# Four blocks of P in flight, half of the second token sums moved into the first products, and a later start for the sample tiles

## The chip, the cores and the metric

The kernel runs on one core of a Trainium2 chip. The metric is the device time of one execution in microseconds (us). The core has five engines with their own instruction queues: TensorE (PE in the profile, with the weight loads apart as PEld), VectorE (DVE), ScalarE (ACT), GpSimd (POOL) and SyncE (SP, which issues the transfers). Every engine takes its instructions in the order of the program, so one that waits holds up all that stand behind it.

## The reference

One layer of an encoder is computed for 1024 prompt tokens and 32 sample tokens with the same weights. Cut to what matters here:

```
h = x @ w_in                                  # q,k,v, indexer, retention q,k,v,gate, two gates
score = sum_h w[t,h] relu(q_idx . k_idx)      # then the top 256 keys of a query are kept
p = softmax(q k^T / 8 + bias, kept keys only) # 8 heads of 64
a = p @ v
o, S = retention_chunk(rotary(q), rotary(k), v, S)        # 8 heads, recurrent over chunks
m = sigmoid(g_a) * (a @ w_pa) + sigmoid(g_r) * (r @ w_pr)
x1 = layer_norm(alpha * x + m @ w_o)
h = silu(x1 @ w_gate) * (x1 @ w_up)           # D_FF = 2816 = 22 blocks of 128
y = layer_norm(alpha * x1 + h @ w_down)
```

## The kernel before

Nearly every product is done in three passes: an operand is split into a rounded high part and the low remainder, and the products high x high, high x low and low x high are summed. The helper `split` makes the two parts (L148 the high part on ACT, L152 the low part on POOL or DVE). In a `unit`, one 128x1024 piece of a weight is loaded and split.

The 1056 tokens are nine tiles, tiles 0 to 7 of 128 prompt tokens and tile 8 with the 32 sample tokens. The stages follow each other: the first projections with the indexer; keys and queries; the retention (`ret_job`); the sixteen gate blocks (`g_jobs`), into which the attention is woven; the merge (`c_jobs`); the output projection; the feed-forward (`u_plain`, then `u_jobs` with `products`); and the last projection.

TensorE's order is written out by hand. A planner, `Weave`, keeps a clock `W.t` of its own and planned busy times of ACT, DVE and POOL. A main generator yields its matmuls one by one; generators in `W.sides` are given the turn when the planned time at which they asked to go on has come. The order of the other engines is made by a scheduler from the data dependences, in a list schedule.

The three places of the change:

- **Retention.** `ret_job` projects a tile (q, k, v of two heads) and spawns `ret_tile`, which rotates q and k on POOL (L574 to L577, into `qk`), transposes both on PE (L580, L581), and goes on with products L593, L604, L607, L610 and the transposes L642. The time `t_ev` at which the projection should be evicted starts its plan. For the sample tile the projection is evicted by `merge_s` (ACT, then DVE L207 into `qkv`).
- **Attention.** `front` writes, for each head and tile, the scores (L788, L790), adds bias and mask (P<-TB,mask on POOL L778; sum and maximum on DVE L792), takes the exponential (ACT L802) and normalizes (DVE L805). `back` goes through blocks (head, group of two tiles, key block kb): it transposes a block of P into a PSUM bank (L842, L843; L849 for the sample tile), splits it into `ph` (ACT L148) and `pl` (DVE L152), and multiplies both with V (L866, L867; L872). `it - ia` is the number of blocks transposed and not yet multiplied. PE's PSUM tiles `m` come from a pool of six banks, `g` from one of two. The matmuls of the gate blocks (L172, `g<-xh`) are the main stream between them; the last gate block waits until the attention is done.
- **Feed-forward.** Blocks of the hidden layer are made two by two with seven products of sums instead of eight plain ones (`Quad` for the weights, `sums` for the tokens, `products` for the matmuls). The tokens are two halves of 528 columns, each in two parts `u` of 264. `sums(u)` makes, for four slices k, the sums `tq[1]`, `tq[2]`, `tq[3]` (tiles T) and `T4` (which takes the place of B12, a tile x) from B11, B12, B21, B22. `sums(0)` and `sums(1)` stand around the plain products of the first two blocks (`u_plain`, with SiLU on ACT L1168 and the product `sg` on DVE L1170). Then `products(q, 0, ...)` and `products(q, 1, ...)` run for each of 20 steps: seven groups of twelve matmuls, z = 0 to 6 (L1218). Group z = 0 is copied by ACT (L1222, `e1`) before group z = 4 may go on in the same bank; z = 1, 2, 3 are taken by DVE (L1224, L1226, L1228).

Of the kernel before, what the change touches and what calls it, by code (L numbers as in the profile page):

```python
# [104 lines left out]
def body(ctx, tc, nc, a):  # L105
# [20 lines left out]
    def f32(ap):  # L126
        return ap.bitcast(F32)
# [550 lines left out]
    def ret_job():  # L678
        for p in range(4):
            for t in range(9):  # L680
                if p == 3 and t == 1:
                    ring2.close()
                    st["hA"] = Open("headA")
                if p == 3 and 1 <= t < 6:
                    load_head(0, t - 1)
                if p < 3 and t < 4:
                    load_pair(p + 2, t)
                    W.on("v", 1.2, W.on("a", 0.95, W.t + 0.5))
                qkv = rp.tile([128, 512], F32, name="qkv", bufs=3)
                src = yield from nat_tile(units[p + 1], t, rp, qkv)  # L690
                t_ev = W.t + 0.2
                if t < 8:
                    nc.scalar.activation(qkv, src, AF.Copy)
                    t_ev = W.on("a", 0.5, W.t)
                    src = qkv
                W.spawn(ret_tile(p, t, src, t_ev))
            units.pop(p)
# [4 lines left out]
    def g_jobs():  # L702
        w = blk(unit(a["wT"][19], ring1, lo_eng="dve"))
        for b in range(16):
            cur = w
            if b < 15:
                w = blk(unit(a["wT"][20 + b], ring1, lo_eng="dve" if b < 1 else "pool"))
# [43 lines left out]
    def attention():  # L751
# [62 lines left out]
        def back():  # L814
# [4 lines left out]
            while ia < len(items):  # L819
                opts = []  # L820
                if it < len(items) and it - ia < 3:
                    h, g, kb = items[it]
                    opts.append((P_at.get((h, min(2 * g + 1, 8)), W.t + 0.3), 1))
# [9 lines left out]
                if is_t:  # L833
# [3 lines left out]
                    pt = mbank()  # L837
                    if g < 4:
                        ph = ap.tile([128, 256], F32R, name="ph", bufs=3)
                        pl = ap.tile([128, 256], F32R, name="pl", bufs=3)  # L840
# [5 lines left out]
                    else:  # L846
# [4 lines left out]
                        ph = ap.tile([128, 5, 2, 32], F32R, name="ps", bufs=1)  # L851
# [264 lines left out]
    def sums(u):  # L1116
        s = slice(u * SUB, (u + 1) * SUB)
        for k in range(4):
            a_, b_, c_ = (st["up"].tile([128, SUB], F32, name=nm, bufs=2) for nm in ("e1", "u2", "u3"))
            d_ = st["up"].tile([128, SUB], F32, name="ts", bufs=1)  # L1120
            nc.gpsimd.tensor_tensor(d_, f32(B21[0][:, k, s]), f32(B21[1][:, k, s]), op=ALU.add)
# [16 lines left out]
            nc.vector.tensor_tensor(c_, d_, c_, op=ALU.subtract)  # L1138
            cut(T4, c_)

    def u_plain():
# [29 lines left out]
        sums(1)  # L1171
# [80 lines left out]
    def u_jobs():  # L1252
        nxt = st["quad"]
        for x, (m, f) in enumerate(seq):
# [11 lines left out]
            yield from products(q, 0, sg, m == 0, {})  # L1266
# [209 lines left out]
```

## Time and profile before

| what | value |
|---|---|
| time, median of 3 runs | 1900.14 us (1900.13 to 1900.14) |
| the profiled execution | 1900.51 us |
| its span, first to last instruction | 1898.9 us |
| TensorE busy | 1859.0 us, 98% of the span |
| DVE, ACT, POOL busy | 68%, 38%, 40% |
| granted TensorE clock, mean | 0.994 of full |

The rows further down come from one profiled execution. A timeline row gives start and length in us, engine, line, operation, written tile <- read tiles, shapes and, in brackets, how long the engine had been idle and what ended the wait. Matmuls overlap, so the distance between two starts, not the length, tells what one costs.

### The profile page before, as it was taken

To read this page: it belongs to the slowest core of one execution; us is meant where nothing else is said; L and a number is where in the kernel's file an instruction comes from. 1 tells how busy PE (TensorE), PEld (TensorE's weight loads), DVE (VectorE), ACT (ScalarE), POOL (GpSimd) and SP (SyncE) were. 2 spreads that over 40 slices of the span, in tenths; PEclk is the share of its full clock that TensorE was granted. 3 is DMA by queue.
4 is the path that set the end of the run, shared out by engine and by line. 5 is a ranking of instruction groups with operands and counts; after the bars stand their busy time and mean duration, and the time that the engine had idled before them with its cause. 6 is when DMAs were issued, how large, how long until landed. Compare 5 with 4: busy or idle time off the path is not lost. (4 is left out here: it accounts for less than half of the span.)

```text
span 1898.9 us, 31028 instructions
## 1 busy us (share of the span) xinstructions
PE 1859.0 (98%) x11361; PEld 1688.2 (89%) x11361; DVE 1298.4 (68%) x2693; ACT 715.1 (38%) x1495; POOL 751.8 (40%) x787
## 2 busy tenths in 40 slices
PE   8999999999999999999999999899999999999998
PEld 8999899787888999998999879899999999877776
DVE  4599889999995776676533378754555555476667
ACT  5443322423333555555522255432333332432212
POOL 5445633455545544543321133243343333462211
PEclk9999999999999999999999999999999999999999
DMA  5335742223334756551845662212222222642212
GB/s 189 113 128 196 266 138 86 65 73 98 87 86 125 195 144 171 143 145 52 273 146 155 186 199 84 67 68 67 80 96 71 75 82 90 203 165 89 83 40 91
DMA packets 154367, 233.11 MB, mean 123 GB/s; under 512 B 18960, under 2 KB 118280, under 8 KB 154216
## 3 DMA queue, kind: packets, MB, share of 16 engines
q1 hardware_dynamic: 147736, 223.03, 37.6%
q10 hardware_dynamic: 6480, 8.11, 1.3%
q8 instruction: 89, 1.46, 0.3%
q14 instruction: 62, 0.51, 0.1%
HBM read 164.79 MB, written 67.48 MB: 122 GB/s over the span
## 5 line engine op out<-in xcount | busy, mean ns | idle before, releaser
L152 POOL TENSOR_TENSOR wlo<-raw,whi 128x1024 fp32r<-128x1024 f32 (+2 forms) x83 | 196.1, 2367 | 337.8 <-ACT whi L148 295.2
L148 ACT ACTIVATE whi<-raw 128x1024 fp32r<-128x1024 f32 (+1 forms) x158 | 137.1, 881 | 183.8 <-PE m L1218 33.7
L172 PE MATMUL g<-xh,whi 128*128 128x384 f32 (+1 forms) x600 | 198.2, 330 | 0.0
L172 PE MATMUL g<-xl,whi 128*128 128x384 f32 (+1 forms) x600 | 198.1, 330 | 0.0
L172 PE MATMUL g<-xh,wlo 128*128 128x384 f32 (+1 forms) x600 | 197.9, 330 | 0.0
L377 DVE MAX8 m<-sc 128x8 f32<-128x384 f32 (+6 forms) x209 | 182.2, 874 | 4.7
L378 DVE MATCH_REPLACE8 sc<-m,sc 128x384 f32<-128x384 f32 (+6 forms) x209 | 180.0, 862 | 0.1
L778 POOL TENSOR_TENSOR P<-TB,mask 128x512 f32<-128x512 f32 (+3 forms) x112 | 99.1, 913 | 120.9 <-PE m L842 98.3
L172 PEld LDWEIGHTS g<-xl,whi 128*128 128x128 f32 x600 | 113.5, 189 | 3.0 <-issue 0.9
L172 PEld LDWEIGHTS g<-xh,wlo 128*128 128x128 f32 x600 | 113.5, 189 | 2.4 <-issue 0.5
L172 PEld LDWEIGHTS g<-xh,whi 128*128 128x128 f32 x600 | 113.5, 189 | 2.2
L1315 DVE TENSOR_TENSOR yo<-m,yo 128x512 f32<-128x512 f32 x128 | 85.4, 686 | 43.5 <-PE m L172 42.1
L1218 PE MATMUL m<-T,whi 128*128 128x264 f32 x624 | 114.6, 283 | 0.0
L172 PE MATMUL g<-whi,xl 128*128 128x512 f32 x256 | 104.9, 410 | 0.0
L172 PE MATMUL g<-whi,xh 128*128 128x512 f32 x256 | 104.4, 408 | 0.0
L172 PE MATMUL g<-wlo,xh 128*128 128x512 f32 x256 | 104.4, 408 | 0.0
L1218 PEld LDWEIGHTS m<-T,whi 128*128 128x128 f32 x624 | 96.6, 188 | 0.0
L172 PE MATMUL m<-rT,whi 128*128 128x384 f32 (+1 forms) x384 | 90.7, 322 | 0.0
L1218 PE MATMUL m<-T,wlo 128*128 128x264 f32 x312 | 88.6, 284 | 0.0
L1218 PE MATMUL g<-x,whi 128*128 128x264 f32 x416 | 79.2, 287 | 5.6 <-ACT e L1222 5.6
L1218 PE MATMUL m<-x,whi 128*128 128x264 f32 x416 | 78.5, 287 | 1.2 <-DVE u L1226 0.7
L152 DVE TENSOR_TENSOR wlo<-raw,whi 128x512 fp32r<-128x512 f32 (+1 forms) x81 | 69.6, 872 | 14.0 <-ACT whi L148 13.1
(333 smaller groups left out, 5493.4 us busy)
## 6 DMA issues: line engine op xcount, KB each, us to landing
raw<-wT SPq DMA_DIRECT2D x33, 512.0 KB, 3.7
raw<-w_gate SPq DMA_DIRECT2D x22, 512.0 KB, 3.4
raw<-w_up SPq DMA_DIRECT2D x22, 512.0 KB, 3.4
hd<-sg SPq DMA_DIRECT2D x22, 512.0 KB, 3.2
raw<-w_down SPq DMA_DIRECT2D x22, 512.0 KB, 3.5
raw<-hd SPq DMA_DIRECT2D x22, 512.0 KB, 3.6
raw<-wr SPq DMA_DIRECT2D x16, 512.0 KB, 4.2
ml<-mtd SPq DMA_DIRECT2D x16, 512.0 KB, 4.5
```

The costliest lines, as they stand in the source:

```text
L148: nc.scalar.activation(hi, src, AF.Copy)
L152: e.tensor_tensor(lo, src, f32(hi), op=ALU.subtract)
L172: nc.tensor.matmul(out, lhsT=l, rhs=r, start=i == 0, stop=i == m - 1)
L377: nc.vector.max(m8[0:n], v)
L378: nc.vector.match_replace(v, m8[0:n], v, TAKEN)
L778: nc.gpsimd.tensor_tensor(pp[0:n, n0:n0 + nn], TB[0:n, b0 + n0:b0 + n0 + nn], masks[t][0:n, n0:n0 + nn], op=ALU.add)
L1218: nc.tensor.matmul(o, lhsT=w[l][:, k, :], rhs=b[r][:, k, s], start=z < 4 and k == 0 and j == 0, stop=k == 3 and j == 2, skip_group_check=True)
L1315: nc.vector.tensor_tensor(y, src, y, op=ALU.add)
```

## The change

```diff
@@ ret_job, after the projection of tile t
                     src = qkv
+                else:
+                    t_ev += 1.6
                 W.spawn(ret_tile(p, t, src, t_ev))
@@ g_jobs
-                w = blk(unit(a["wT"][20 + b], ring1, lo_eng="dve" if b < 1 else "pool"))
+                w = blk(unit(a["wT"][20 + b], ring1, lo_eng="dve" if b < 2 else "pool"))
@@ attention, back()
-                if it < len(items) and it - ia < 3:
+                if it < len(items) and it - ia < 4:
                     h, g, kb = items[it]
-                    opts.append((P_at.get((h, min(2 * g + 1, 8)), W.t + 0.3), 1))
+                    opts.append((max(P_at.get((h, min(2 * g + 1, 8)), W.t + 0.3), tev.get(it - 3, 0.0) - 0.6), 1))
...
                     pt = mbank()
+                    pp = ap.tile([128, 512], F32R, name="ph", bufs=4)
                     if g < 4:
-                        ph = ap.tile([128, 256], F32R, name="ph", bufs=3)
-                        pl = ap.tile([128, 256], F32R, name="pl", bufs=3)
+                        ph, pl = pp[:, 0:256], pp[:, 256:512]
...
-                        ph = ap.tile([128, 5, 2, 32], F32R, name="ps", bufs=1)
+                        ph = pp[:, 0:320].rearrange("p (b i c) -> p b i c", b=5, i=2)
@@ sums
-    def sums(u):
+    def sums(u, ks=range(4)):
         s = slice(u * SUB, (u + 1) * SUB)
-        for k in range(4):
+        for k in ks:
             a_, b_, c_ = (st["up"].tile([128, SUB], F32, name=nm, bufs=2) for nm in ("e1", "u2", "u3"))
-            d_ = st["up"].tile([128, SUB], F32, name="ts", bufs=1)
-            nc.gpsimd.tensor_tensor(d_, f32(B21[0][:, k, s]), f32(B21[1][:, k, s]), op=ALU.add)
...
-            nc.vector.tensor_tensor(c_, d_, c_, op=ALU.subtract)
+            whole(b_, B21)
+            nc.vector.tensor_tensor(c_, b_, c_, op=ALU.subtract)
             cut(T4, c_)
@@ u_plain, behind the plain products
-        sums(1)
+        sums(1, range(2))
@@ u_jobs
-            yield from products(q, 0, sg, m == 0, {})
+            yield from products(q, 0, sg, m == 0, {z: (lambda k=z: sums(1, [k + 1])) for z in (1, 2)} if x == 0 else {})
             yield from products(q, 1, sg, m == 0, hooks)
```

The sample tile's `ret_tile` is planned 1.6 us later; the low part of the weight piece of gate block 2 (piece 21) goes from POOL to DVE; four blocks instead of three may be transposed ahead, the fourth not before the splits of the block three earlier are planned to end, less 0.6 us; the sum over B21 is made on DVE (`whole`) instead of POOL; and slices k = 2 and 3 of `sums(1)` are written behind groups z = 1 and z = 2 of the first products.

**POOL at the fourth sample tile.** The rows are POOL's rotation of the last sample tile (`qk_6609`) and the low parts `wlo` of gate weights that stand next to it. Before:

```order
L574 TENSOR_TENSOR qk_6609<-qkv_6514,rot_6604 32x256
L575 TENSOR_TENSOR t2_6610<-qkv_6514,rot_6604 32x256
L152 TENSOR_TENSOR wlo_6819<-raw_6816,whi_6818 128x1024
L576 TENSOR_TENSOR qk_6609<-qk_6609,t2_6610 32x4x32
L577 TENSOR_TENSOR qk_6609<-qk_6609,t2_6610 32x4x32
L152 TENSOR_TENSOR wlo_6948<-raw_6945,whi_6947 128x1024
```

The same place in the changed kernel:

```order
L574 TENSOR_TENSOR qk_6609<-qkv_6514,rot_6604 32x256
L575 TENSOR_TENSOR t2_6610<-qkv_6514,rot_6604 32x256
L576 TENSOR_TENSOR qk_6609<-qk_6609,t2_6610 32x4x32
L577 TENSOR_TENSOR qk_6609<-qk_6609,t2_6610 32x4x32
L152 TENSOR_TENSOR wlo_6921<-raw_6918,whi_6920 128x1024
```

The weight's low part that stood inside the rotation is gone from POOL's queue; it is now made by DVE.

**PE at the end of the attention.** The rows are the transposes of blocks of P into PSUM tiles `m`, and their products with V; the block transposed into `m_N` is split into `ph_(N+1)`. Before, for the last head:

```order
L842 MATMUL m_10921<-ident_65,P_10732 128x128
L843 MATMUL m_10921<-ident_65,P_10796 128x128
L866 MATMUL m_10928<-ph_10900,V_9876 128x256
L867 MATMUL m_10928<-pl_10901,V_9876 128x256
L842 MATMUL m_10931<-ident_65,P_10732 128x128
L843 MATMUL m_10931<-ident_65,P_10796 128x128
L866 MATMUL m_10928<-ph_10909,V_9876 128x256
L867 MATMUL m_10928<-pl_10910,V_9876 128x256
L842 MATMUL m_10940<-ident_65,P_10732 128x128
L843 MATMUL m_10940<-ident_65,P_10796 128x128
L866 MATMUL m_10928<-ph_10922,V_9876 128x256
```

In the changed kernel, from the last matmul of gate block 15 on (the last but one of the sixteen):

```order
L172 MATMUL g_10681<-xh_141,wlo_10174 128x288
L844 MATMUL m_10745<-ident_65,P_10534 128x128
L845 MATMUL m_10745<-ident_65,P_10587 128x128
L868 MATMUL m_10694<-ph_10685,V_9739 128x256
L869 MATMUL m_10694<-ph_10685,V_9739 128x256
L844 MATMUL m_10753<-ident_65,P_10534 128x128
L845 MATMUL m_10753<-ident_65,P_10587 128x128
L868 MATMUL m_10694<-ph_10700,V_9739 128x256
L869 MATMUL m_10694<-ph_10700,V_9739 128x256
L844 MATMUL m_10761<-ident_65,P_10534 128x128
L845 MATMUL m_10761<-ident_65,P_10587 128x128
L868 MATMUL m_10694<-ph_10711,V_9739 128x128
```

Between a block's transposes and its first product stood the products of two other blocks, and now stand those of three. Behind the last matmul of that gate block 85 rows of the attention were left, and now 41 are (the whole list of PE's rows was counted).

**ACT ahead of the first products.** The rows are the high parts of the second token sums (T, x), of the hidden block for the sample tokens (`hs`), and the copy `e1` of group z = 0. Before:

```order
L148 ACTIVATE hs_13240<-sg_13268 128x32
L148 ACTIVATE T30_13533<-u2_13888 128x264
L148 ACTIVATE T30_13533<-u2_13908 128x264
L148 ACTIVATE T20_13531<-u3_13889 128x264
L1222 ACTIVATE e1_13970<-g_13966 128x264
L148 ACTIVATE T20_13531<-u3_13909 128x264
L148 ACTIVATE x10_01_12441<-u3_13889 128x264
L1231 ACTIVATE sg_13944<-g_13966 128x264
```

In the changed kernel:

```order
L148 ACTIVATE hs_13080<-sg_13108 128x32
L1223 ACTIVATE e1_13764<-g_13760 128x264
L148 ACTIVATE T10_13369<-e1_13793 128x264
L148 ACTIVATE T30_13373<-u2_13794 128x264
L148 ACTIVATE T20_13371<-u3_13795 128x264
L1243 ACTIVATE sg_13738<-sg_13738 128x264
L1232 ACTIVATE sg_13738<-g_13760 128x264
```

The copy now follows `hs` directly; the three high parts that stood between them come later.

## Rows read from the trace of the kernel before

**Rows 1.** The page, busy time of each engine.
```profile
PE 1859.0 (98%) x11361; PEld 1688.2 (89%) x11361; DVE 1298.4 (68%) x2693; ACT 715.1 (38%) x1495; POOL 751.8 (40%) x787
```
**Rows 2.** Waits of PE, whole span (total, times, longest).
```profile
PE m L580 <- POOL qk L577: 5.8, 3, 2.8
PE g L1218 <- ACT e L1222: 5.6, 1, 5.6
...
PE m L1218 <- DVE u L1226: 1.1, 4, 0.5
```
**Rows 3.** Timeline of PE at 448 us, one sample tile.
```profile
448.32 0.24 PE L580 MATMUL m<-ident,qk 32*128 32x32 f32 x1 [1.91 <-POOL qk L577]
...
449.36 0.40 PE L172 MATMUL g<-wlo,xh 128*128 128x512 f32 x1
449.59 0.39 PE L172 MATMUL g<-whi,xl 128*128 128x512 f32 x1
```
**Rows 4.** Timeline of POOL at 585 us, the last sample tile.
```profile
584.86 2.35 POOL L152 TENSOR_TENSOR wlo<-raw,whi 128x1024 fp32r<-128x1024 f32 x1 [0.26 <-ACT whi L148]
587.17 0.45 POOL L576 TENSOR_TENSOR qk<-qk,t 32x128 f32<-32x128 f32 x1
```
**Rows 5.** Waits of PE from 626 to 879.5 us, the attention.
```profile
PE m L867 <- DVE pl L152: 2.4, 5, 0.9
PE m L866 <- ACT ph L148: 0.8, 1, 0.8
PE m L788 <- DVE mx L792: 0.5, 2, 0.2
```
**Rows 6.** Stretches: length, busy us (instructions) PE, PEld, DVE, ACT, POOL; clock, DMA.
```profile
879.53:900.85 21.32, 16.75 (x93) 13.28 (x91) 16.46 (x51) 12.87 (x33) 3.67 (x3) 0.84 0.14 40
...
883.80:890.60 6.80, 5.94 (x21) 4.71 (x22) 5.48 (x18) 2.83 (x7) 0.20 (x1) 0.50 0.30 87
...
900.85:904.25 3.40, 3.40 (x12) 3.40 (x12) 0.40 (x2) 0.22 (x1) 0.00 (x0) 0.50 0.10 22
...
1164.00:1204.40 40.40, 40.40 (x335) 40.40 (x334) 39.10 (x91) 20.14 (x46) 14.33 (x10) 1.00 0.21 79
...
1204.40:1210.40 6.00, 5.99 (x50) 5.77 (x48) 4.09 (x4) 2.52 (x5) 5.85 (x5) 1.00 0.00 0
...
1204.43:1223.47 19.04, 12.97 (x87) 12.45 (x85) 13.78 (x29) 6.61 (x16) 6.57 (x6) 0.82 0.08 28
...
1214.90:1221.70 6.80, 5.25 (x22) 4.94 (x23) 4.79 (x13) 3.00 (x8) 0.75 (x1) 0.50 0.07 21
```
**Rows 7.** Timeline of POOL and DVE at 736 us, in the attention.
```profile
736.44 2.56 POOL L152 TENSOR_TENSOR wlo<-raw,whi 128x1024 fp32r<-128x1024 f32 x1 [3.46 <-ACT whi L148]
...
736.66 2.35 DVE L800 TENSOR_TENSOR mx<-mx 128x1 f32<-128x1 f32 x1
```
**Rows 8.** Timeline of PE and DVE at 897 us, blocks of the last head.
```profile
897.03 0.27 PE L843 MATMUL m<-ident,P 128*128 128x128 f32 x1
...
897.49 0.27 PE L843 MATMUL m<-ident,P 128*128 128x128 f32 x1
...
897.76 0.88 DVE L152 TENSOR_TENSOR pl<-m,ph 128x256 fp32r<-128x256 f32 x2 [0.38 <-ACT ph L148]
...
898.24 0.39 PE L867 MATMUL m<-pl,V 128*128 128x256 f32 x1
```
**Rows 9.** Timeline of DVE, ACT and PE, 1206 to 1216 us, the first products.
```profile
1206.43 1.50 DVE L1138 TENSOR_TENSOR u<-ts,u 128x264 f32<-128x264 f32 x1 [1.91 <-POOL ts L1121]
...
1212.10 0.42 DVE L1170 TENSOR_TENSOR sg<-m,sg 128x264 f32<-128x264 f32 x1
1212.44 0.42 DVE L1124 TENSOR_TENSOR u<-x,x 128x264 f32<-128x264 f32 x1
...
1215.56 0.37 ACT L1222 ACTIVATE e<-g 128x264 f32<-128x264 f32 x1
...
1215.99 0.81 PE L1218 MATMUL g<-x,whi 128*128 128x264 f32 x2 [5.60 <-ACT e L1222]
```

## The prediction

> **What bounds the kernel now.** I read the page first: TensorE is busy 1859.0 of 1898.9 us [rows 1], so the time can fall only where PE waits, or where it works at half clock. The waits of PE name the places [rows 2]: three waits for the rotated sample tile (5.8 us, the longest 2.8), one wait of 5.6 us for the copy `e1` at the first products, and small ones of 1.1 us there. The waits of the attention come in two stretches: 3.7 us in the long one, where gate matmuls stand between the blocks [rows 5], and 4.6 us of idle time in the 21.3 us at its end, where none are left [rows 6]. The stretches also give the granted clock [rows 6]: it stands at 0.50, the lower of the two levels (1.2 instead of 2.4 GHz), in 883.8 to 890.6, in 900.85 to 904.25 and in 1214.9 to 1221.7 us, each time behind one of these waits. So a wait costs its length and often some us at half speed behind it. The change touches just these places.
>
> **Sample tiles of the retention.** The sum of the three waits is 5.8 us; the longest is 2.8 [rows 2], the middle one 1.91 [rows 3], so the first is 1.1. The wait ends when POOL has rotated `qk`. Putting the plan 1.6 us later moves PE's other work ahead of the transposes. In the second of these tiles 22 projection matmuls instead of 16 and two more transposes stand between the end of the sample projection and its transposes (counted in the order); at 0.23 us each [rows 3] the six are 1.4 us, with the transposes about 1.5, and 0.4 us of the 1.91 stay. In the first tile four matmuls and one product L593 come ahead, about 1.2 us against 1.1: nothing stays. In the last tile POOL's `wlo` of 2.35 us stood between the second and the third step of the rotation, and its third step began only at 587.17 [rows 4]; this row is gone from there, and eight more matmuls stand ahead, so the 2.8 us go wholly. The low part now costs DVE about 1.2 us (an estimate: half of POOL's 2.35), hidden as long as the product that waits for DVE stands more than that behind its turn; the order keeps some 3.6 us of other matmuls between L593 and L604, as before. Later tiles are spaced as before within 0.1 us at the shortest, so I add no new wait. Term: 5.8 - 0.4 = **5.4 us**, between 4.2 (0.6 us left in each of two tiles, 0.4 in a third) and 5.8.
>
> **First products.** From their start to the start of the second part (`u` = 1) they took 19.04 us. At full clock 50 matmuls take 6.00 us, 0.12 each, so the 84 of one part are 10.1 us: 8.9 us were lost there (the wait of 5.6, some 0.5 of small waits, and 2.8 at half clock) [rows 2, 6]. The cause is a chain of late work. DVE was busy 39.10 of the 40.40 us ahead [rows 6], and came 7.5 us late to the last `sg`, at 1212.10, when PE had ended its product at about 1204.6; on the way it also waited 1.91 us for POOL's `ts` [rows 9]. Behind `sg` the order gives ACT three high parts of the second sums, which wait for DVE in turn, before `e1`, which came at 1215.56 [rows 9].
>
> After the change `e1` stands right behind `hs`. Ahead of the last `sg` DVE has as many rows as before, 94 against 95: the eight sums over B21 replace what of slices 2 and 3 stood there. Counted with the distance of two starts, 0.34 us [rows 9], they are about 35 us of work; in the trace the same rows kept DVE busy some 45 us (39.1 up to 1204.4, and 5.8 of the 7.7 us to the last `sg`), because DVE instructions stretch while POOL works (the row of 1.50 us with POOL's name beside it is a 0.42 us one [rows 9]). Five of POOL's ten rows there [rows 6] are `ts`, so I let 6 of these 10 us stay: DVE, which begins at about 1165.5, reaches the last `sg` at about 1206.7, `e1` comes at 1207.5, and group z = 4 needs it at 1204.4 + 4 x 1.45 = 1210.2. If all 10 us stay, it comes at 1211.2 and PE waits 1.0 us. Then slices 2 and 3: 24 DVE rows and what they wait for end near 1216.9, and the second part reads the last slice of `tq[2]` at 1204.4 + 10.1 + 1.45 + 1.1 = 1217.1. There the cover is thin. ACT must first copy the second part's `e1`, ready at 1216.1, before the last high part; I put 0.6 us of new waiting here, and up to 2.5 if DVE is late by all the 10 us. Without such waits the clock has no reason to fall. Term: 8.9 - 0.6 = **8.3 us**, between 5.4 (1.0 and 2.5 us come back) and 8.9.
>
> The Trainium skill bears on this step: its page "SBUF — State Buffer" (Who interferes with whom) says that a DVE instruction with two SBUF inputs contends with a GpSimd instruction that reads SBUF, and that the second to issue is blocked. By that rule the sum over B21 is no safer on DVE than on POOL, and POOL's remaining weight sums could hold it up; the trace agrees that a DVE row with SBUF inputs alone can stand 2.35 us where POOL works [rows 7]. It would move this term towards 5.4.
>
> **Attention, its end.** From the last gate matmul to the end PE was busy 16.75 of 21.32 us: 4.57 us idle. In the two stretches at half clock it was busy 5.94 and 3.40 us, of which half, 3.0 and 1.7, is the price of the clock [rows 6]. Together 9.3 us. From a block's second transpose to its product with the low part it was 1.21 us [rows 8], and before the change a block had only about 0.9 us of PE work in between. After it, 41 instead of 85 rows lie behind the last gate matmul, no scores among them, and three blocks' work (about 1.3 us) stands between transpose and product. A block follows the next on PE in 0.46 us and costs DVE 0.44 [rows 8], so the splits just keep up. I leave 1.2 us for its last, short blocks, and expect no fall of the clock. Term: **8.0 us**, between 5.0 (the longer fall returns) and 9.3.
>
> **Attention, its long part.** The 3.7 us of waits [rows 5] come where POOL splits a gate weight: 2.56 us of POOL, a DVE row of one column stretched to 2.35 beside it, and the splits `pl` behind it late [rows 7]. Thirteen such POOL rows stay. A fourth block in flight gives a block more cover where there was least of it; over all blocks the median of PE work between transpose and product goes only from 3.05 to 3.26 us. The price of such a hit is not known in the new order. It can be anything from nothing (all 3.7 us won) to 1.5 us more than now (two more hits of the size of the longest ones, 0.8 and 0.9 us). Term: **1.8 us**, half.
>
> **The sum.** 5.4 + 8.3 + 8.0 + 1.8 = 23.5 us. The profiled execution took 1900.51 us, its span is 1.6 us shorter, and the median of the runs is 0.4 us below it; I subtract from the median: 1900.1 - 23.5 = **1876.6 us**. All low ends together give 13.1 us (1887.0), all high ends 27.7 us (1872.4).
>
> **The rivals.**
>
> The attention gives nothing back (chance 0.15): the fourth block changes the order, new hits by POOL's splits take the place of the old ones, and the end keeps its waits and its falls of the clock. For it speaks that POOL's rows are all still there; against it that 44 rows have left the bare end. Then 13.7 us of gain remain: 1886.4.
>
> The end of the attention stays dense but the clock falls in it anyway (0.15). Between the two falls the clock was full for ten us of transposes and products, since the mean of 0.84 over the end is just the first fall, and it fell again right behind them [rows 6]; so the trace doesn't exclude it. As a mechanism of this kernel: transposes are half of these rows; if they keep the clock no better than idle time, one or two falls return, at 1.7 to 3.0 us, and 1876.6 becomes 1878.3 to 1881.3. The Trainium skill, "TensorE: Matmul & The Clock Gate" (Part 4: PE-mode transpose), says that a transpose doesn't count as busy in the same way; by that rule this rival holds.
>
> The second sums are late (0.12): DVE is late by all that POOL took from it, and the products of the second part wait for slice 3. 3.5 us come back, 1879.5 (2.9 above the forecast), a little more if the clock falls again.
>
> The fourth block takes a PSUM bank (0.03), and the kernel is slower. Six banks hold two score tiles, up to two sums over V and now four transposed blocks. If the scores have to wait for the fourth block's splits, the nearest row is 0.23 us each (0.5 us in two waits for DVE's `mx` [rows 5]); with 112 score pieces that is 26 us against 23.5: 1902. It decides from about 100 of the 112 on. Against it: the fourth is held back in the plan, and in the order a bank's next use lies at least as far behind as before.
>
> No change that can be measured (0.03): the waits only move, 1900.
>
> **How the numbers follow.** The forecast itself has 0.52. Its own range is 1873 to 1880; the clock rival and the late sums lie within 1878 to 1882, the first rival at 1886. A range of 1871.5 to 1887 leaves out some 0.15: the two last rivals and a gain beyond the high ends. Less than 0.2% (3.8 us) can hardly be told from no change here. Faster by more has 0.94, the same 0.03, slower 0.03.
>
> **What would show it.** Right: no wait of PE for `qk` above 0.6 us; POOL's last rotation without a split inside; `e1` before 1210 us on the old clock and no wait of over a us in the first products; about 8 us instead of 21 from the gate matmul at the attention's bare end to its last product; clock 1.00 through both places. Wrong: a wait for T or `x` in the second part of the first products, waits for `pl` in the long part above 4 us together, or score products that wait for `mx` many times.

## The result and the profile after

The changed kernel takes 1877.4 us (median of four runs, 1875.5 to 1878.5); the kernel before took 1900.1 us beside it. The ratio on record is 0.9864, with a 95% interval of 0.9847 to 0.9882, so it is faster; the two medians alone give 0.9880, which lies in the interval. The forecast was 1876.6 us. One execution of run 5 below, 2082.6 us at a mean clock of 0.82, was slow and counts in no ratio. The profiled execution took 1878.54 us, with a span of 1876.4 us, 22.5 less than the 1898.9 before.

The page, busy time of each engine (answers to [rows 1]):

```profile
PE 1852.4 (99%) x11361; PEld 1681.8 (90%) x11361; DVE 1293.0 (69%) x2702; ACT 713.4 (38%) x1495; POOL 741.5 (40%) x778
```

PE is busy 6.6 us less though it executes the same number of instructions. Most of that is half clock that is gone: half of PE's busy time at 0.50 was 7.3 us before and is 1.7 now. The other 15.9 of the 22.5 us are waiting. The waits of PE over the whole span (total, times, longest; answers to [rows 2]):

```profile
PE m L306 <- ACT xh L148: 4.3, 1, 4.3
...
PE m L869 <- DVE ph L152: 1.3, 1, 1.3
PE m L844 <- DVE mx L794: 1.1, 1, 1.1
...
PE m L580 <- POOL qk L577: 0.6, 1, 0.6
PE m L1219 <- ACT T L148: 0.5, 1, 0.5
```

The wait of 5.6 us for `e1` is no longer there, and of the three waits for `qk` (5.8 us) one of 0.6 is left. New are a wait of 1.3 us for a split of P, one of 1.1 us for `mx`, and 0.5 us for T. The stretches of the changed kernel (columns as in [rows 6]) show where the half clock went:

```profile
754.06:757.47 3.41, 3.41 (x15) 3.31 (x15) 0.90 (x3) 1.10 (x4) 2.92 (x4) 0.50 0.01 2
879.34:886.17 6.83, 6.14 (x49) 5.37 (x48) 3.88 (x12) 5.05 (x14) 2.38 (x1) 1.00 0.35 107
1187.97:1198.10 10.13, 10.13 (x86) 10.12 (x85) 9.06 (x24) 5.03 (x13) 1.59 (x2) 1.00 0.16 53
```

The second row is the bare end of the attention: 6.83 us with 0.7 us of idle time and a clock of 1.00, against 21.32 us with 4.57 idle, 6.8 of them at 0.50, and 3.4 more at 0.50 right behind, before. It also holds fewer rows, 49 against 93. The third is the way from the first products to the start of their second part: 10.13 us without a gap, against 19.04. The first row is new: 3.41 us at half clock in the attention's long part. Before, three stretches were at half clock (6.8, 3.4 and 6.8 us [rows 6]) between the kernel's start and its last microseconds; this one is all that is left there.

The places of [rows 4] and [rows 9] again, in the changed kernel. POOL rotates the last sample tile without a pause, and the low part of a weight comes later:

```profile
580.59 0.72 POOL L574 TENSOR_TENSOR qk<-qkv,rot 32x256 f32<-32x256 f32 x1 [2.21 <-PE m L604]
581.28 0.73 POOL L575 TENSOR_TENSOR t<-qkv,rot 32x256 f32<-32x256 f32 x1
582.09 0.45 POOL L576 TENSOR_TENSOR qk<-qk,t 32x128 f32<-32x128 f32 x1
582.51 0.45 POOL L577 TENSOR_TENSOR qk<-qk,t 32x128 f32<-32x128 f32 x1
585.22 2.38 POOL L152 TENSOR_TENSOR wlo<-raw,whi 128x1024 fp32r<-128x1024 f32 x1 [2.26 <-ACT whi L148]
```

And DVE, ACT and PE in the first products:

```profile
1191.07 0.42 DVE L1171 TENSOR_TENSOR sg<-m,sg 128x264 f32<-128x264 f32 x1
...
1191.65 0.37 ACT L1223 ACTIVATE e<-g 128x264 f32<-128x264 f32 x1
...
1201.43 0.39 PE L1219 MATMUL m<-T,mh 128*128 128x264 f32 x1 [0.55 <-ACT T L148]
...
1202.12 0.39 PE L1219 MATMUL m<-T,mh 128*128 128x264 f32 x1 [0.31 <-DVE T L152]
```

The first products now start at 1187.97 instead of 1204.43, 16.5 us earlier; on the old clock `e1` comes at 1208.1, before group z = 4 needs it at 1210.2, and PE doesn't wait. It waits later, 0.86 us in two waits for the last slice of `tq[2]`. By the distance of the starts these two cost 1.3 us: the start of the second part comes 25.4 us earlier than before (1198.10 against 1223.47), the row at 1202.12 only 24.0 (1226.16 before).

The new wait in the long part, with the fall of the clock behind it, has this history on POOL, DVE and PE:

```profile
748.80 2.39 POOL L152 TENSOR_TENSOR wlo<-raw,whi 128x1024 fp32r<-128x1024 f32 x1 [5.67 <-ACT whi L148]
...
749.75 1.59 DVE L807 TENSOR_SCALAR P<-P,mx 128x256 f32<-128x256 f32 x1
...
752.49 1.27 DVE L152 TENSOR_TENSOR ph<-m,ph 128x256 fp32r<-128x256 f32 x4
...
752.96 0.38 PE L869 MATMUL m<-ph,V 128*128 128x256 f32 x1 [1.31 <-DVE ph L152]
```

POOL splits a gate weight for 2.39 us. Beside it, a DVE row over 256 columns takes 1.59 us, though the same operation over 640 columns took 0.54 us at 736 us in the kernel before. The low parts of P behind it are late, and PE waits 1.31 us. It is the pattern of [rows 7] at another place.

### The profile page after: what moved, and what is told of

Its sections match the earlier page's. It is cut to its first block, busy times and chain, and to the rows that moved or that the text cites. A ratio compares the mean times of both kernels' runs of the same rounds, so it can differ in the third digit from the quotient of the medians.

```text
span 1876.4 us, 30959 instructions
## 1 busy us (share of the span) xinstructions
PE 1852.4 (99%) x11361; PEld 1681.8 (90%) x11361; DVE 1293.0 (69%) x2702; ACT 713.4 (38%) x1495; POOL 741.5 (40%) x778
## 5 line engine op out<-in xcount | busy, mean ns | idle before, releaser
L172 PE MATMUL g<-xl,whi 128*128 128x384 f32 (+1 forms) x600 | 198.7, 331 | 0.0
L172 PE MATMUL g<-xh,wlo 128*128 128x384 f32 (+1 forms) x600 | 198.0, 330 | 0.0
L172 PE MATMUL g<-xh,whi 128*128 128x384 f32 (+1 forms) x600 | 197.4, 329 | 0.0
L172 PEld LDWEIGHTS g<-xl,whi 128*128 128x128 f32 x600 | 113.2, 189 | 3.1 <-issue 0.9
L172 PEld LDWEIGHTS g<-xh,wlo 128*128 128x128 f32 x600 | 113.3, 189 | 2.7 <-issue 0.5
L172 PEld LDWEIGHTS g<-xh,whi 128*128 128x128 f32 x600 | 113.1, 189 | 2.6
L172 PE MATMUL g<-wlo,xh 128*128 128x512 f32 x256 | 105.3, 411 | 0.0
L172 PE MATMUL g<-whi,xh 128*128 128x512 f32 x256 | 105.0, 410 | 0.0
L172 PE MATMUL g<-whi,xl 128*128 128x512 f32 x256 | 103.4, 404 | 0.0
L172 PE MATMUL m<-rT,whi 128*128 128x384 f32 (+1 forms) x384 | 90.8, 322 | 0.0
L1199 POOL TENSOR_TENSOR raw<-raw,qs 128x512 f32<-128x512 f32 x20 | 31.9, 1596 | 145.5 <-DVE wlo L152 95.0
L794 DVE CUSTOM_DVE_ANT_0 P<-m,P 128x512 f32<-128x512 f32 (+3 forms) x112 | 59.0, 532 | 38.6 <-PE m L792 34.3
L152 DVE TENSOR_TENSOR ph<-m,ph 128x256 fp32r<-128x256 f32 (+2 forms) x176 | 62.0, 374 | 28.7 <-ACT ph L148 27.7
```

The source lines that it names most:

```text
L152: e.tensor_tensor(lo, src, f32(hi), op=ALU.subtract)
L172: nc.tensor.matmul(out, lhsT=l, rhs=r, start=i == 0, stop=i == m - 1)
L794: nc.vector.tensor_tensor_reduce(out=pp[0:n, n0:n0 + nn], in0=L[0:n, 0:nn], in1=pp[0:n, n0:n0 + nn], scale=1.0, scalar=-3e38, op0=ALU.add, ...
L1199: nc.gpsimd.tensor_tensor(a12, a12, self.s2, op=ALU.subtract)
```

## The experiments

Twelve runs were made, of eleven other kernels and of the changed one again, each in up to five rounds beside the kernel before. That one took 1898.7 to 1907.2 us in the 37 runs of these rows, with medians of 1903.1, 1902.7 and 1903.8 us, so differences from the kernel before are given against the median of the same row. Runs 1 to 4, 5 to 8 and 9 to 12 are one row each; a comparison across rows is given by the times and by the ratios, which need not agree. All ratios are to the kernel before, with 95% intervals.

**Run 1: the sample tiles alone.** The kernel before with

```diff
+                else:
+                    t_ev += 1.6
                 W.spawn(ret_tile(p, t, src, t_ev))
-                w = blk(unit(a["wT"][20 + b], ring1, lo_eng="dve" if b < 1 else "pool"))
+                w = blk(unit(a["wT"][20 + b], ring1, lo_eng="dve" if b < 2 else "pool"))
```

> Only the later plan of the sample tiles and gate piece 21's low part on DVE. If the three parts of the change are independent: the three waits for qk (5.8 us) shrink to 0.6, nothing else moves, 1900.1 - 5.2 = 1894.9 us. Rival, the parts lean on each other: the 30 gate matmuls that are pulled ahead of the sample tiles are missing in the attention (860 instead of 890 stand inside it in the order), and with three blocks in flight 97 instead of 84 rows lie behind the last gate matmul. At the 9.3 us that the bare end cost for 84 rows, 0.11 each, 1.4 us come back: about 1896.3, and a longer bare end with the same falls of the clock.

Measured: 1893.9 us, 9.3 below before; ratio 0.9951 (0.9937 to 0.9964). This is more than either theory gave. The waits of PE:

```profile
PE m L845 <- DVE P L807: 4.2, 1, 4.2
...
PE m L580 <- POOL qk L577: 0.6, 1, 0.6
```

The waits for `qk` shrink as expected, by 5.2 us. The end of the attention keeps its idle time (one wait alone takes 4.2 us), with less half clock than in the profile of before:

```profile
875.21:878.62 3.41, 2.81 (x10) 2.62 (x11) 3.10 (x14) 2.99 (x7) 1.37 (x2) 0.50 0.20 44
```

Here 3.4 us stand at 0.50 where before has 10.2, and in the first products 3.4 us where before has 6.8. As half of PE's busy time, these falls cost 2.9 instead of 7.3 us. So 4.4 of the 9.4 us by which the two spans differ were gained at places that the edit doesn't touch, and the falls of one kernel vary between executions: the runs of the kernel before have mean clocks of 0.991 to 0.995.

But the profile of before may also show too few falls at the sample tiles. In the five other kernels of this study in which the sample tiles' plan is that of before (runs 2, 3, 5, 6 and 11), each profile shows half clock at a wait for `qk`, from its last half microsecond on or behind it. Stretches of run 3 and the wait ahead of the first:

```profile
448.08 0.25 PE L580 MATMUL m<-ident,qk 32*128 32x32 f32 x1 [1.90 <-POOL qk L577]
```

```profile
449.03:452.44 3.41, 3.41 (x11) 2.61 (x10) 3.41 (x8) 0.69 (x3) 0.00 (x0) 0.50 0.40 147
588.98:595.80 6.82, 6.19 (x20) 5.68 (x21) 4.46 (x7) 2.06 (x7) 4.67 (x7) 0.50 0.65 218
```

Runs 3 and 5 had both falls, 10.2 us at half clock, which cost 4.8 and 4.6; runs 2, 6 and 11 had one of 3.4 us, which cost 1.6 to 1.7. The mean over the five is 2.9 us. The one profile of before on which the prediction was worked out has the same waits [rows 2, 3] and no fall behind them. With the 5.2 us of the waits themselves that makes 8.1 us, inside the measured interval of 6.9 to 12.0. How much of the 9.3 us the sample tiles gave is not shown.

**Run 2: the fourth block alone.** The kernel before with

```diff
-                if it < len(items) and it - ia < 3:
+                if it < len(items) and it - ia < 4:
...
-                    opts.append((P_at.get((h, min(2 * g + 1, 8)), W.t + 0.3), 1))
+                    opts.append((max(P_at.get((h, min(2 * g + 1, 8)), W.t + 0.3), tev.get(it - 3, 0.0) - 0.6), 1))
...
+                    pp = ap.tile([128, 512], F32R, name="ph", bufs=4)
```

and `ph`, `pl` taken from `pp` as in the change.

> Only the fourth block in flight, its hold-back and the common tile for ph and pl. Independent parts: the attention's 9.2 us at the end less 0.6, and about 1 us in the long part, 1900.1 - 9.6 = 1890.5 us; 11 rows behind the last gate matmul (84 before), no clock below full there. Rival: the gain at the end is taken back by new hits of POOL's weight splits in the long part, as the one with a clock fall at 754 us in the changed kernel (3.0 us): 1893 to 1895.

Measured: 1895.5 us, 7.7 below before; ratio 0.9962 (0.9949 to 0.9975). The bare end behaves as expected: no half clock there, and one wait of 0.39 us. But the merge behind it now waits for the attention's result:

```profile
893.06 0.92 PE L872 MATMUL m<-ph,V 128*128 128x64 f32 x5 [0.39 <-DVE ph L152]
911.32 0.44 PE L172 MATMUL m<-aT,whi 128*128 128x384 f32 x1 [1.21 <-DVE aT L152]
914.37 0.45 PE L172 MATMUL m<-aT,whi 128*128 128x384 f32 x1 [1.74 <-DVE aT L152]
```

These 2.9 us are a loss at a place that neither theory named; they don't stand in the whole change. The time is that of the rival (1893 to 1895), for another reason: no fall of the clock stands in the long part, whose small waits (0.2 to 0.4 us each, most of them for `ph`) make some 2 us in place of 3.7 [rows 5], a wait of 1.2 us at 626.5 us left out that before has at 625. Whether the 2.9 us come from the order or from transfers that were slow in that execution wasn't tried.

**Run 3: the token sums alone.** The kernel before with

```diff
-            d_ = st["up"].tile([128, SUB], F32, name="ts", bufs=1)
-            nc.gpsimd.tensor_tensor(d_, f32(B21[0][:, k, s]), f32(B21[1][:, k, s]), op=ALU.add)
...
+            whole(b_, B21)
...
-        sums(1)
+        sums(1, range(2))
...
-            yield from products(q, 0, sg, m == 0, {})
+            yield from products(q, 0, sg, m == 0, {z: (lambda k=z: sums(1, [k + 1])) for z in (1, 2)} if x == 0 else {})
```

> Only the second token sums: B21 summed on DVE, slices 2 and 3 inside the first products. Independent parts: the first products' start to the start of their second part takes about 10.3 us instead of 19.0, two small waits for T, and 0.6 us new at the first ordinary products: 1900.1 - 8.0 = 1892.1 us. Rival: the start of this stage differs here, since the attention and merge ahead are as before and DVE may come to it later; then e1 is late again by up to 3 us and the clock falls: 1895 to 1897.

Measured: 1895.8 us, 7.4 below before; ratio 0.9965 (0.9953 to 0.9978). No wait for `e1` is left, and the two for T are there (0.54 and 0.31 us). The stage does here what it does in the whole change.

The three parts alone sum to 9.3 + 7.7 + 7.4 = 24.4 us; the whole change gained 26.1 in run 9. The product of the three ratios is 0.9878, give or take 0.0023 by their intervals; the whole has 0.9860 (0.9846 to 0.9873). Within what is measured the parts add up.

**Run 4: no hold-back.** The changed kernel with

```diff
-                    opts.append((max(P_at.get((h, min(2 * g + 1, 8)), W.t + 0.3), tev.get(it - 3, 0.0) - 0.6), 1))
+                    opts.append((P_at.get((h, min(2 * g + 1, 8)), W.t + 0.3), 1))
```

> The changed kernel without the hold-back of the fourth block (it may be transposed as soon as P is there). If the hold-back is what keeps the six PSUM banks from running short: score products wait for mx many times, 2 to 10 us slower than the changed kernel's 1877.4, with waits of L790 and L844 for mx. Rival: the banks were never short, and the freer order only draws the end in (1 row instead of 40 behind the last gate matmul): the 0.5 us at the end go, 1876 to 1877.

Measured: 1890.7 us; ratio 0.9934 (0.9922 to 0.9947), 13 us above the changed kernel. The banks do run short. PE's waits in the attention, and one of them on PE, DVE and POOL:

```profile
PE m L790 <- DVE mx L794: 10.5, 7, 1.9
PE m L845 <- DVE mx L794: 1.6, 3, 0.8
```

```profile
671.50 0.42 PE L790 MATMUL m<-KS,QS 128*32 128x512 f32 x1 [1.89 <-DVE mx L794]
```

```profile
667.99 2.86 DVE L807 TENSOR_SCALAR P<-P,mx 128x896 f32<-128x896 f32 x1
...
670.76 0.68 DVE L794 CUSTOM_DVE_ANT_0 P<-m,P 128x512 f32<-128x512 f32 x1
...
667.99 2.37 POOL L152 TENSOR_TENSOR wlo<-raw,whi 128x1024 fp32r<-128x1024 f32 x1 [3.97 <-ACT whi L148]
```

PE has transposed four blocks one behind the other. Their splits, and the sum over an earlier score tile (L794, which frees its bank), stand on DVE behind a normalization of 2.86 us; the next score matmul has no bank and waits 1.89 us. What makes the normalization so long stands beside it: POOL's split of a gate weight begins at the same time. The same row in the changed kernel, where no split runs:

```profile
668.50 0.69 DVE L807 TENSOR_SCALAR P<-P,mx 128x896 f32<-128x896 f32 x1
```

Four of the seven waits of L790 are of this kind, 1.89 us each. So the rival of the prediction that a fourth block takes a bank is a real mechanism, and the held-back start of the fourth block keeps it away; but its longest waits need POOL's split as well. Whether the hold-back is needed when DVE makes the splits wasn't tried.

**Run 5: the sums over B21 on DVE, nothing split.** The kernel before with the first two pieces of the diff of run 3 alone.

```diff
-            nc.gpsimd.tensor_tensor(d_, f32(B21[0][:, k, s]), f32(B21[1][:, k, s]), op=ALU.add)
+            whole(b_, B21)
```

> The kernel before with the sums over B21 on DVE, and nothing split: all four slices still stand ahead of the first products. My reason (what is queued ahead of the copy e1 decides): in ACT's order four high parts of slice 3 and 2 still stand between hs and e1, and DVE has four rows more ahead of the last sg; the wait of 5.6 us for e1 stays at 5 to 7 us and the time is that of before, within 2 us. Rival (POOL's late sum ts is what holds DVE): the wait for ts of 1.9 us and the stretching of DVE's rows by POOL go, e1 comes some 4 us earlier, and 3 to 6 us are gained.

Measured: 1902.4 us, ratio 0.9998 (0.9988 to 1.0007): no change. ACT's timeline shows why:

```profile
1210.87 0.23 ACT L148 ACTIVATE hs<-sg 128x32 fp32r<-128x32 f32 x1 [0.26 <-DVE sg L1169]
1212.16 0.42 ACT L148 ACTIVATE T<-e 128x264 fp32r<-128x264 f32 x1 [1.06 <-DVE e L1129]
1213.89 0.42 ACT L148 ACTIVATE T<-u 128x264 fp32r<-128x264 f32 x1 [1.31 <-DVE u L1131]
1214.58 0.77 ACT L148 ACTIVATE T<-u 128x264 fp32r<-128x264 f32 x2 [0.26 <-DVE u L1131]
1215.26 0.37 ACT L1221 ACTIVATE e<-g 128x264 f32<-128x264 f32 x1
```

`hs` is ready at 1210.87, yet `e1` comes 4.4 us later, since four high parts stand between them and wait for DVE in turn. PE waits 3.6 us for `e1` and 1.9 us for `u` behind it, 5.5 together.

**Run 6: the split alone.** The kernel before with the last two pieces of the diff of run 3; the sums over B21 stay on POOL.

```diff
-        sums(1)
+        sums(1, range(2))
...
-            yield from products(q, 0, sg, m == 0, {})
+            yield from products(q, 0, sg, m == 0, {z: (lambda k=z: sums(1, [k + 1])) for z in (1, 2)} if x == 0 else {})
```

> The kernel before with slices 2 and 3 of the second sums behind groups z = 1 and z = 2 of the first products, the sums over B21 still on POOL. My reason: e1 stands right behind hs and loses its wait; it gains nearly what both halves together gained (about 7 us below before on this chip), less at most 2 us for DVE waiting on POOL inside the products. Rival: POOL's sums are late inside the products, T and x of slices 2 and 3 come some us late, and only 3 to 4 us are gained.

Measured: 1895.5 us, ratio 0.9966 (0.9953 to 0.9978), the same as run 3 with both. PE waits 1.0 us for `u` between 1190 and 1215 us, in place of the two waits for T. The gain of this stage is that of the order in which ACT comes to `e1`; on which engine the sums over B21 are made doesn't count within these intervals (2.4 us to either side).

**Run 7: all low parts of gate weights on DVE.** The changed kernel with

```diff
-                w = blk(unit(a["wT"][20 + b], ring1, lo_eng="dve" if b < 2 else "pool"))
+                w = blk(unit(a["wT"][20 + b], ring1, lo_eng="dve"))
```

> The changed kernel with the low parts of all gate weights on DVE, so that POOL splits no weight during the attention. If POOL's splits cause the waits that are left in the long part (1.3 us at 753 with the fall of the clock behind it, 0.6 at 628, 1.1 at 670): they go, 3 to 4 us faster than the changed kernel. Rival: the 13 splits are 15 us of work more for DVE in the attention, which it would have to do among the splits of P; waits for ph and mx grow, 3 to 10 us slower than the changed kernel.

Measured: 1872.5 us (1871.7 to 1874.3), ratio 0.9842 (0.9829 to 0.9856). Against the changed kernel (run 9, in another row) that is 5 us faster by the times, which don't overlap (1876.1 to 1878.6 there), and 3.4 us by the ratios, whose intervals do. It is the fastest kernel of the study. PE's order is the same row by row. From 626 to 880 us, the changed kernel first and then this one:

```profile
626.00:880.00 254.00, 250.60 (x1692) 238.75 (x1690) 182.04 (x657) 143.08 (x379) 114.87 (x112) 0.99 0.53 141
```

```profile
626.00:880.00 254.00, 253.53 (x1733) 242.37 (x1732) 189.91 (x678) 147.62 (x390) 95.85 (x103) 1.00 0.54 143
```

PE's idle time falls from 3.4 to 0.5 us and the clock is full. DVE from the first score to the last product of the attention, in the changed kernel, in this one, and the splits `wlo` of this one alone (length, busy us (rows) of DVE; clock, DMA):

```profile
611.60:886.24 274.64, 195.50 (x702) 0.99 0.55 147
```

```profile
611.85:881.20 269.35, 199.61 (x712) 1.00 0.57 150
...
611.85:881.20 269.35, 13.29 (x10) 1.00 0.57 150
```

The stretch is 5.3 us shorter. Ten of the thirteen moved splits stand in it and take 13.3 us, yet DVE is busy only 4.1 us more: its other 702 rows take 186.3 instead of 195.5 us, 9.2 less, now that POOL splits no weight beside them. One split costs 1.3 us on DVE and 2.4 on POOL.

**Run 8: the fourth block later.** The changed kernel with

```diff
-tev.get(it - 3, 0.0) - 0.6
+tev.get(it - 3, 0.0) - 0.0
```

> The changed kernel with the fourth block held back 0.6 us longer (until the splits of the block three earlier are planned to end, not 0.6 us before). Run 4 without any hold-back waited for mx in a dozen places. If the planned time draws a line between bank waits and cover: the waits for mx of 1.1 and 0.4 us that are left go, but 55 instead of 40 rows lie behind the last gate matmul but one block and the end waits 0.5 to 1 us more; in all the same within 2 us. Rival: three blocks were the cause of the end, and with a fourth that comes later the end gets its waits and its half clock back, 3 to 5 us slower than the changed kernel.

Measured: 1880.9 us, ratio 0.9884 (0.9870 to 0.9897), 3 us slower than the changed kernel by the times and 4.6 by the ratios, whose intervals overlap. The waits for `mx` at the transposes and the scores go, and waits for splits take their place: `ph` 3.0 us in seven waits, against 1.3 in one. Its end, 870 to 890 us, at full clock:

```profile
PE m L869 <- DVE mx L806: 0.8, 1, 0.8
PE m L869 <- DVE ph L152: 0.6, 1, 0.6
PE m L868 <- ACT ph L148: 0.3, 1, 0.3
```

The size is that of the rival, the half clock that it named isn't there, nor anywhere else in the attention. From the first score to the last product PE idles 5.1 us, against 4.1 in the changed kernel. This 1 us does not make up the 3, so the cause of the rest stays open. Both values tried beside 0.6 are slower; earlier costs banks, and that later costs cover is read off the kind of its waits.

**Run 9: the changed kernel again**, without an edit.

> The changed kernel itself once more, next to the others of this row, since the kernel before varies here between 1899 and 1907 us. Independent parts: the ratio of 0.986 comes again, 1877 us within 2. If its spread comes from clock falls that come and go behind waits: the mean clock of its runs lies between 0.997 and 0.999, against 0.991 to 0.995 before, and the longer runs are those with the lower clock.

Measured: 1877.7 us (1876.1 to 1878.6), ratio 0.9860 (0.9846 to 0.9873). The waits are those of the first profile to within 0.01 us in the attention (1.31 at 753, 1.10 at 670), and the half clock behind the first of them is there again. The longest run, 1878.6 us, had a mean clock of 0.998, the others 0.999.

**Run 10: piece 21 back on POOL.** The changed kernel with

```diff
-                w = blk(unit(a["wT"][20 + b], ring1, lo_eng="dve" if b < 2 else "pool"))
+                w = blk(unit(a["wT"][20 + b], ring1, lo_eng="dve" if b < 1 else "pool"))
```

> The changed kernel with the low part of gate piece 21 back on POOL; the sample tiles stay 1.6 us later. My step for the last sample tile: POOL's 2.35 us stand inside the rotation again, and the eight gate matmuls ahead (1.8 us) cover 1.8 of the 2.8 us; PE waits 1.0 us for qk there, 1 to 1.5 us slower than the changed kernel, up to 3 if the clock falls behind it. Rival: the later plan alone covers the wait, no difference.

Measured: 1881.7 us, ratio 0.9881 (0.9867 to 0.9894), 4 us slower than run 9 beside it, where 1 to 3 were expected. POOL and PE:

```profile
582.62 2.40 POOL L152 TENSOR_TENSOR wlo<-raw,whi 128x1024 fp32r<-128x1024 f32 x1 [0.33 <-ACT whi L148]
584.97 0.45 POOL L576 TENSOR_TENSOR qk<-qk,t 32x128 f32<-32x128 f32 x1
```

```profile
585.88 0.25 PE L580 MATMUL m<-ident,qk 32*128 32x32 f32 x1 [1.22 <-POOL qk L577]
```

The split stands inside the rotation again and PE waits 1.22 us, as the step on the last sample tile gave (1.0). Of the 4 us the waits for `qk` make 1.7 (2.0 us together, 0.3 in run 9), and a wait of 1.1 us in the last projection (L172 for `smp`), which the edit doesn't touch, is part of the rest. Run 11 has the other half: with piece 21 on DVE and the old plan the last tile waits 0.35 us, but the first two still 1.1 and 1.9. So both edits of this part are needed. The profile of this run has the wait of 1.31 us at 754 us too, and no half clock behind it: 1.00 from 754.06 to 760.90. A fall behind the same wait comes in one profile and not in another.

**Run 11: all low parts on DVE, the rest as before.** The kernel before with

```diff
-                w = blk(unit(a["wT"][20 + b], ring1, lo_eng="dve" if b < 1 else "pool"))
+                w = blk(unit(a["wT"][20 + b], ring1, lo_eng="dve"))
```

> The kernel before (three blocks in flight, all else as it was) with the low parts of all gate weights on DVE. If POOL's splits cause the waits of the attention's long part whatever the number of blocks: of the 3.7 us there at least 2.5 go, with the 0.9 and 0.8 us waits at 741 us and the falls of the clock behind them, and the 2.8 us at the last sample tile shrink as in the change: 5 to 8 us faster than before. Rival: three blocks leave DVE no room, and the 14 splits more cost what they give; the same within 2 us.

Measured: 1896.1 us, 7.8 below before; ratio 0.9958 (0.9944 to 0.9971), in the range of the first theory. But its step on the long part was too simple. The waits from 626 to 879.5 us:

```profile
PE m L866 <- ACT ph L148: 1.4, 2, 1.1
PE m L867 <- DVE pl L152: 1.2, 2, 0.9
```

Of the 3.7 us [rows 5], 2.6 are left, at another place (703 us), with half clock behind them; the wait for the last `qk` is 0.35 us instead of 2.8. With four blocks and the same splits on DVE only 0.7 us were left (run 7), so POOL's splits are not the only cause of the waits where three blocks are in flight.

**Run 12: run 7 with two further steps.** The changed kernel with

```diff
-                w = blk(unit(a["wT"][20 + b], ring1, lo_eng="dve" if b < 2 else "pool"))
+                w = blk(unit(a["wT"][20 + b], ring1, lo_eng="dve"))
...
-                    t_ev += 1.6
+                    t_ev += 2.4
...
-{z: (lambda k=z: sums(1, [k + 1])) for z in (1, 2)}
+{z: (lambda k=z: sums(1, [k + 2])) for z in (0, 1)}
```

> The changed kernel with all low parts of gate weights on DVE (25 to 30 us below before when tried), the sample tiles another 0.8 us later, and slices 2 and 3 of the second sums behind groups z = 0 and z = 1. If waits are what is left: the 0.6 us for qk and the 0.9 us for T in the first products go, 1.5 us less, 1870 to 1872. Rival: the sums of slice 2 now stand ahead of DVE's take of z = 1, PE waits there instead, the same or 1 us more.

Measured: 1878.5 us, ratio 0.9863 (0.9850 to 0.9877), 6 us slower than run 7 by the times and 4 by the ratios, and no faster than the changed kernel in its own row (run 9). The waits for `qk` and T are gone, and a larger one has come, on DVE and PE:

```profile
1193.74 0.42 DVE L1133 TENSOR_TENSOR u<-u,u 128x264 f32<-128x264 f32 x1
1194.09 0.42 DVE L1227 TENSOR_TENSOR u<-m,u 128x264 f32<-128x264 f32 x1
```

```profile
1194.57 0.66 PE L1219 MATMUL m<-x,whi 128*128 128x264 f32 x2 [4.14 <-DVE u L1227]
```

The rows of both slices stand ahead of DVE's take of group z = 2 (L1227), and the group that adds to the same bank waits 4.14 us for it. Half clock follows for 3.4 us. The direction is the rival's; its size (at most 1 us) was far too small.

## Why the prediction held, point by point

**What bounds the kernel.** Right: the time fell where PE waited or worked at half clock, and elsewhere by half a microsecond at most.

**Sample tiles (5.4 us).** In the two profiles the waits fall from 5.8 to 0.6 us, 5.2; what is left is in the second tile, as said, and run 10 gives the step on the last tile. The term may be too small: it counted the waits alone because no fall stood behind them in the one profile, while five other profiles show falls there worth 2.9 us on the mean. Run 1 measured 9.3 (6.9 to 12.0), but 4.4 us between the two profiles come from falls at other places.

**First products (8.3 us).** From the rows 19.04 - 10.13 - 1.3 = 7.6; run 3 measured 7.4 (4.2 to 8.9). `e1` came at 1208.1 for the predicted 1207.5, the new waiting was 0.86 us for 0.6, at a cost of 1.3. It came as the wait for T in the second part that the prediction had named as a sign of being wrong; none of its other signs of that kind came. Run 6 shows that the cause was the queue ahead of `e1`, and run 5 that POOL's `ts`, of which the prediction made a part of the delay, was none that mattered. The Trainium skill's rule from "SBUF — State Buffer" (Who interferes with whom), which spoke for a worse term here, makes the sum over B21 no safer on DVE than on POOL; runs 3 and 6, with one ratio, agree, and the fall of the term towards 5.4 didn't come. The Trainium skill's page "SBUF — State Buffer" (Who interferes with whom) also says that a DVE instruction in a two-port mode, which it allows `tensor_scalar`, contends with GpSimd, and that the one that issues later is fully blocked for the whole of the other. A row of the attention agrees, though no run shows its mode: the DVE row of 1.59 us at 749.75 ends at 751.34, 0.15 us behind POOL's split (748.80 + 2.39 = 751.19).

**Attention, its end (8.0 us).** 9.3 us were lost there, and 0.7 are now: 8.6 from the rows. Run 2, with the fourth block alone, has the clean end too, and run 1, with three blocks, has not. The size leans on the one profile, though: its falls there cost 4.7 us, and four of the five other profiles with three blocks (runs 1, 5, 6 and 11) show 1.4 to 1.7. The rival that the clock falls anyway fell: 49 rows from 879.34 to 886.17, 20 of them transposes, kept 1.00. So the rule of the Trainium skill, "TensorE: Matmul & The Clock Gate" (Part 4: PE-mode transpose), that a transpose doesn't count as busy in the same way, decided nothing here; no run shows transposes alone.

**Attention, its long part (1.8 us).** Wrong in size. From 626 us on, the waits of 3.7 us became 3.4, and a fall of the clock worth 1.7 came behind one of them; a wait of 1.3 us at 625 us, ahead of that stretch, is gone. Together nothing was gained. The step that failed is the half that I took between the ends; the hits moved, as the first rival said of the whole attention. What was not weighed is that they could be removed: with four blocks most of them go when POOL splits no gate weight (run 7).

**The PSUM bank (0.03).** The mechanism is real (run 4, 13 us), and what spoke against it, the hold-back, is what prevented it. POOL's split, beside which its longest waits arise, was not in the step.

**The sum.** By the rows 5.2 + 7.6 + 8.6 + 0 = 21.4 of the 22.5 us of the spans. The same PE rows in both traces give a second count. From the first transposes of the retention (L580) to those behind the output projection (L1026), 795.9 us became 780.2: 15.7 us, where the prediction's three terms there make 15.2. From the start of the first products to the last row of L1218, 420.1 us became 413.4: 6.7 us instead of 8.3, the waits for T and a new one of 0.9 us for `u` at 1362 us taken off. The long part gave nothing, yet its stretch came out above the forecast; that it is more than the 13.8 us of the rows is probably because a wait costs more than its idle time, as the two for T do (1.3 us for 0.86). The waits at the kernel's start (L306), which the change doesn't touch, fell from 5.6 to 4.9.

Part of the closeness is luck. In the rows of the experiments the kernel before had medians of 1902.7 to 1903.8, and the change gained 26 us there (run 9). The median of 1900.1 that the prediction subtracted from lies at the fast end of what that kernel does, and the one profile that it was worked out on had no fall at the sample tiles and long ones at the attention's end. That these errors cancelled is argued from the profiles and not measured apart.

## What to carry to other kernels

Read what an engine's queue holds ahead of the instruction that is waited for: here three high parts that nobody needed yet stood ahead of the one that PE needed, and moving work to another engine gave nothing while reordering gave all. When more work is put in flight, look for the resource that it takes (PSUM banks) and hold it back by that; both sides of the right value cost 3 to 13 us. Look at what POOL does beside a DVE row that stands in the way: 0.69 us became 2.86 beside a split (run 4), and taking the splits from POOL gave 3 to 5 us (run 7). A wait of PE costs its length and, in some executions, half clock on top (here 1.7 us behind waits of 1.3 and 1.9 us), so look at more than one profile before costing it.

## What was unexpected on the hardware

The same wait at the same place brings half clock in one execution and none in another: 1.31 us at 753 to 755 us was followed by 3.4 us at half clock in two of the three profiles with it, and 1.9 us at 448 us in four of the six profiles that have it. These profiles are of different kernels, but for two of the changed one. The kernel before, with more such waits, varied over 8.5 us in 37 runs; the changed kernel varied over 2.5 us in the four of run 9 and run 7 over 2.6 in five, though so few runs span less by themselves.

A low part of a 128x1024 weight took 1.2 us on DVE (median) and 2.4 us on POOL, and moving thirteen of them onto DVE, the busier engine of the two, made the kernel faster by 5 us (by the times) or 3.4 (by the ratios).
